# Projections from z1 by seven block products in segments 1 to 3 of a hybrid trunk layer

## The chip, the cores and the metric

The kernel runs on one core of one Trainium2 chip. The metric is the device time of one execution in microseconds (us); of several runs the median counts.

## The reference

One layer on 2048 positions of width 1024, with 16 meta positions ahead of them. All in float32.

```python
h = concat([meta, x]); z = rmsnorm(h, norm1_g)
q, fl, iv, og, pin, ga, gb = split(z @ w_in)        # 1024, 1024, 512, 512, 512, 1024, 1024 columns
o_a = hgrn2_mixer(q, fl + b_f, iv, og, lb, head_norm_g)
o_b = pool_mixer(pin, w_pool, pool_scale)
mix = sigmoid(ga) * (o_a @ w_branch_a) + sigmoid(gb) * (o_b @ w_branch_b)
h = h + mix @ w_out
z = rmsnorm(h, norm2_g); u, v = split(z @ w_up)
h = h + (silu(causal_dwconv(u)) * v) @ w_down
return rmsnorm(h)[:, 16:]
```

`hgrn2_mixer` is a gated linear recurrence with 8 heads of 128 x 64 state: f = lb + (1 - lb) sigmoid(fl), S = diag(f) S + (1 - f) i^T, o = S^T silu(q); then an rms norm of o per head and a product with silu(og). `pool_mixer` takes causal means of 2, 4, 8 and 16 positions less the position itself, and a 128 x 128 product per group.

## The kernel before

The sequence is worked in four segments of 512 columns (`SEG`; segment 0 has the 16 meta columns too). Within a segment the stages follow in this order: values (L271), four head pairs (L554), pooling (L590), the per-head norm (L617), the output gate (L637), the branch gates (L655), the out projection (L718), and the MLP with its down product.

**Precision.** Each operand of a product is kept as two halves, hi (the value rounded to fp32r) and lo (the rest), and a product is three passes, hi*hi, hi*lo, lo*hi (`PASS`, L129). Weights come from DRAM as a block of 128 x 1024 (0.5 MB) by `split_weights` (L90): a DMA on SP's queue into a ring of three `raw` tiles, ACT's cast for hi (L96), DVE's subtract for lo (L97), into a ring of three `w` tiles.

**Projections from z1.** `proj` (L131) makes one block of 128 output columns: 8 blocks of K x 3 passes = 24 matmuls of 128x512 into one PSUM bank. Per segment there are 8 for f, 8 for q, 4 for pooling, 4 for the output gate and 16 for the two branch gates.

**A pair of heads** (L554): both f blocks, k = 1 - f, `decays` (L288: products of f over 8 positions, on DVE, with two reciprocals), q's two blocks, the first block of the next pair's f, then `all_scores` (L346: products of q and k with the decays on DVE, small score products `sp` on PE) and `chunks_out` (L385: state products `up`, states `sc`, output `op`).

**After the pairs.** Pool sums `win` and `dt` (L602, L606), a product `pp`, its split `ob`. Then the squares of the output are split (`oss`) and summed per head by `msb` (L626); `ms` (L630) and `rsqrt` (L164, ten operations on an 8 x 512 tile, each needing the one before) give 1/rms, split into `rss` (L633). For each pair p the output gate's projection gives `t` (L643), times `oraw` (L645), times `bc` (L650: rss spread over the partitions by PE, L649), split into `oa` (L651). The branch gates (L655) make per block of 128 columns two projections from z1, 12 matmuls from `oa`, 12 from `ob`, and `mix`.

**The MLP** of segments 1 to 3 already takes two blocks of 128 columns at a time in seven products instead of eight (`q_rest`, L793): z2 has seven column groups of 256 (four quarters and three of their sums), the weights have seven operands (a11, a12, a22 and the sums s1 to s4), each product is 12 matmuls of 128x256 into half of a bank `X` or `Y`. ACT copies half banks aside (`sx`, `sy`, L817 to L828), DVE adds them (L830, L835). The sums s1 to s4 of the MLP's weights are made once, in segment 0, and kept in DRAM.

```python
129  PASS = ((0, 0), (0, 1), (1, 0))
136  for k in range(nk):
137      for i, (wi, xi) in enumerate(PASS):
138          T.matmul(pt[:, :n], lhsT=w[:, wi, (kof + k) * P:(kof + k + 1) * P],
```

The order of the work on each engine comes from a tile scheduler that places the instructions by its own estimates; each engine then runs its list in order. Pools bound how far it can run ahead: `w` 3, `raw` 3, PSUM 5 + 3 banks, wide rows `am` 12, `t` rows 6, x rows 2.

Of the kernel before, what the change touches and what calls it, by code (L numbers as in the profile page):

```python
# [16 lines left out]
P = 128  # L17
# [32 lines left out]
def trunk_layer(ctx: ExitStack, tc: tile.TileContext, x, meta, wts, cst, gf, wpool, out):  # L50
# [93 lines left out]
    def rows_product(src, chunks, nk, consume, between=(), lo=None, hg=HG, on_raw=None):  # L144
# [3 lines left out]
        for k in range(nk):  # L148
# [63 lines left out]
    def norm1_chunk(src, m, off, dst):  # L212
        t = x_row()
        nc.sync.dma_start(out=t[:m], in_=src)
        ss = new_sums(m < P)
        for i in range(2):
            square_sums(ss[:m, i, 0:1], t[:m, i * 512:(i + 1) * 512], m)
        rs = inv_rms(ss, 1)
        V.tensor_scalar(out=t[:m], in0=t[:m], scalar1=rs[:m, 0:1], scalar2=None, op0=ALU.mult)
        return lambda: norm1_transposes(t, m, off, dst)  # L220

    def norm1_transposes(t, m, off, dst):
        for kk in range(0, KB, 4):
            tp = ps.tile([P, 512], F32, name="tp", tag="mm", bufs=MM)
            for j in range(4):
                T.transpose(out=tp[:, j * P:j * P + m], in_=t[:m, (kk + j) * P:(kk + j + 1) * P],
                            identity=ident[:m, :m])
            for j in range(4):
                k = kk + j
                split((dst[k][:, 0, off:off + m], dst[k][:, 1, off:off + m]), tp[:, j * P:j * P + m],  # L230
                      scale=col(C_G1, k))

# [21 lines left out]
    def norm1(s):  # L254

        dst, rest = [], {}

        def load(c):
            rest[c] = norm1_chunk(x[s * SEG + c * P:s * SEG + (c + 1) * P], P, c * P, dst)

        def step(c, ahead):
            if not dst:
                dst.extend(z_plain())
            rest.pop(c)()
            if ahead:
                load(ahead)
        wait = lambda: None
        return ([lambda: load(0), lambda: load(1)],
                [lambda: step(0, 2), lambda: step(1, 3), wait, lambda: step(2, 0), lambda: step(3, 0)], dst)

    def values(s, z1, lo=None, between=()):  # L271
# [244 lines left out]
    t_d = {j0: dram.tile([4, nj // 2, P, 512], F32, name=f"t_d{j0}") for (j0, nj) in GROUPS}  # L516
    for s in range(nseg):
        if s > 0:
            nxt[0] = V_AT
            vt = values(s, z1)  # L520
# [31 lines left out]

        f_next = None
        for p in range(PAIRS):  # L554
            f = f_next if p else wide("f")
            k, q = wide("k"), wide("q")
            for e in range(1 if p else 0, 2):
                forget(p, e, f)
            nxt[0] = 4 * p + 2
            A.activation(out=k, in_=f, func=AF.Identity, scale=-1.0, bias=one)  # L560
            dec = decays(f, 2 * W)
            for e in range(2):
                b = e * W
# [546 lines left out]
```

## Time and profile before

| | |
|---|---|
| median of 3 runs | 3046.56 us (3041.91 to 3046.71) |
| the profiled execution | 3041.42 us, span 3039.7 us |
| mean granted TensorE clock | 0.996 |
| PE (TensorE) busy | 2969.6 us, 98% |
| PE weight loads busy | 2568.6 us, 85% |
| DVE (VectorE) busy | 2187.4 us, 72% |
| ACT (ScalarE) busy | 1360.8 us, 45% |
| DMA | 483.36 MB, 159 GB/s |

An engine's share is its busy time over the span. The shares are means: a stage can be full on an engine whose mean is low. Matmuls overlap each other in the records, so one matmul's own duration says little; the distance of the starts of a long run of them does. The same holds, less, for DVE.

### The profile page before, as it was taken

The numbers are of one execution on the slowest core, as the hardware profiler recorded it, in microseconds if no ns is written. First come the engines' busy times: TensorE is split into PE (matmuls) and PEld (weight loads), VectorE is DVE, ScalarE is ACT, GpSimd is POOL, SyncE is SP. The second block draws the span as 40 slices with busy tenths as digits, with TensorE's granted clock in tenths as the row PEclk, the third lists the DMA queues.
The fourth block names the chain that finished last, engine by engine and source line by source line (L and its number), as shares of the span: only waits on it lengthen the run. The fifth ranks groups of instructions, "written<-read, shape, count | busy, mean of one in ns | idle before, by whom it ended". The sixth has DMA issues, their size and how long they took to land.

```text
span 3039.7 us, 53537 instructions
## 1 busy us (share of the span) xinstructions
PE 2969.6 (98%) x21526; PEld 2568.6 (85%) x21526; DVE 2187.4 (72%) x3754; ACT 1360.8 (45%) x2214; POOL 74.4 (2%) x180
## 2 busy tenths in 40 slices
PE   7999999999999999999999999999999999999998
PEld 6999978888877788899977778799887778889997
DVE  5875357667868735988887853698887884488888
ACT  4443234333533424655554332555464442365555
POOL 1000000000000000000000000000000000000000
PEclk9999999999999999999999999999999999999999
DMA  3112238777632224666552122566664222356664
GB/s 144 64 64 84 84 137 294 263 268 263 237 135 75 76 92 145 224 216 225 196 197 78 64 90 92 189 203 224 213 204 170 71 71 92 116 180 228 216 218 160
DMA packets 198492, 483.36 MB, mean 159 GB/s; under 512 B 19794, under 2 KB 19922, under 8 KB 198244
## 3 DMA queue, kind: packets, MB, share of 16 engines
q1 hardware_dynamic: 198244, 479.95, 46.2%
q8 instruction: 169, 2.77, 0.4%
q14 instruction: 79, 0.65, 0.1%
HBM read 413.81 MB, written 66.06 MB: 158 GB/s over the span
## 4 chain that ended last, share of the span: by engine, by line
PE 82%; DVE 8%; ACT 5%; DMA 3%; issue 1%; SPq 0%; DVEq 0%; ACTq 0%; POOL 0%; POOLq 0%
PE pt L138 34%; PE rp L158 11%; PE dp L894 10%; PE X L793 8%; PE pt L760 8%; PE Y L793 6%; DVE w L97 2%; DMA raw<-in_wts_dram 1%; ACT w L96 1%; PE sp L328 1%; DVE cv L745 1%; DMA raw<-s_d 1%; DVE xt L286 1%; PE op L423 1%; ACT ta L706 0%
## 5 line engine op out<-in xcount | busy, mean ns | idle before, releaser
L97 DVE TENSOR_TENSOR w<-raw,w 128x1024 fp32r<-128x1024 f32 x625 | 760.9, 1220 | 545.6 <-ACT w L96 541.6
L138 PE MATMUL pt<-z,w 128*128 128x512 f32 (+3 forms) x4800 | 949.9, 353 | 0.0
L96 ACT CAST w<-raw 128x1024 fp32r<-128x1024 f32 x629 | 657.8, 1047 | 574.2 <-PE rp L158 162.2
L138 PEld LDWEIGHTS pt<-z,w 128*128 128x128 f32 x4800 | 769.6, 188 | 135.7 <-issue 11.8
L793 PE MATMUL X<-z,w 128*128 128x256 f32 x2484 | 338.6, 284 | 12.5 <-DVE z L123 4.2
L894 PE MATMUL dp<-w,act 128*128 128x512 f32 x1386 | 334.1, 397 | 11.4 <-DVE w L97 5.0
L793 PEld LDWEIGHTS X<-z,w 128*128 128x128 f32 x2484 | 313.9, 191 | 18.3 <-DVE z L123 5.9
L894 PEld LDWEIGHTS dp<-w,act 128*128 128x128 f32 x1386 | 257.7, 189 | 75.3 <-DVE w L97 8.7
L760 PE MATMUL pt<-z,w 128*128 128x256 f32 (+2 forms) x1608 | 253.7, 320 | 0.0
L760 PEld LDWEIGHTS pt<-z,w 128*128 128x128 f32 x1608 | 229.1, 190 | 23.2
L793 PE MATMUL Y<-z,w 128*128 128x256 f32 x1692 | 233.3, 284 | 2.5 <-ACT sy L826 2.3
L793 PEld LDWEIGHTS Y<-z,w 128*128 128x128 f32 x1692 | 214.7, 192 | 5.2 <-ACT sy L826 4.9
L158 PE MATMUL rp<-w,mix 128*128 128x512 f32 (+1 forms) x816 | 190.3, 394 | 0.0
L158 PEld LDWEIGHTS rp<-w,mix 128*128 128x128 f32 (+1 forms) x816 | 147.8, 182 | 40.1 <-issue 4.7
L661 ACT ACTIVATE sg<-pt 128x512 f32<-128x512 f32 (+1 forms) x80 | 41.2, 515 | 238.9 <-PE pt L138 238.9
L745 DVE SCALAR_TENSOR_TENSOR cv<-ub,cs,cv 128x512 f32<-128x512 f32 x176 | 131.4, 747 | 1.7
L902 DVE TENSOR_TENSOR h<-h,dp 128x512 f32<-128x512 f32 x192 | 124.4, 681 | 9.0 <-PE dp L894 8.9
L158 PE MATMUL rp<-w,act 128*128 128x512 f32 x528 | 123.6, 394 | 0.0
L158 PEld LDWEIGHTS rp<-w,act 128*128 128x128 f32 x528 | 98.9, 188 | 22.6
L748 ACT ACTIVATE sg<-cv 128x512 f32<-128x512 f32 x88 | 55.6, 632 | 113.5 <-DVE cv L745 113.3
L158 PE MATMUL rp<-w,z 128*128 128x512 f32 (+1 forms) x408 | 100.3, 404 | 0.0
L793 PE MATMUL X<-z,wa 128*128 128x256 f32 x684 | 95.6, 281 | 1.5 <-DMA wa<-a_d 1.5
(210 smaller groups left out, 3254.1 us busy)
## 6 DMA issues: line engine op xcount, KB each, us to landing
raw<-in_wts_dram SPq DMA_DIRECT2D x349, 512.0 KB, 3.5
raw<-s_d SPq DMA_DIRECT2D x264, 256.0 KB, 3.3
wa<-a_d SPq DMA_DIRECT2D x114, 512.0 KB, 4.9
raw<-in_wts_dram SPq DMA_DIRECT2D x183, 256.0 KB, 3.3
raw<-t_d SPq DMA_DIRECT2D x132, 256.0 KB, 2.9
a_d<-w SPq DMA_DIRECT2D x44, 512.0 KB, 3.7
s_d<-ws SPq DMA_DIRECT2D x44, 512.0 KB, 4.2
t_d<-ws SPq DMA_DIRECT2D x44, 256.0 KB, 2.2
```

The costliest lines, as they stand in the source:

```text
L96: A.copy(out=w[:, 0, :n], in_=raw[:, :n])
L97: (lo or V).tensor_tensor(out=w[:, 1, :n], in0=raw[:, :n], in1=w[:, 0, :n].bitcast(F32), op=ALU.subtract)
L138: T.matmul(pt[:, :n], lhsT=w[:, wi, (kof + k) * P:(kof + k + 1) * P], rhs=src[k][:, xi, c0 + o:c0 + o + n], start=(k == 0 and i == 0), sto ...
L158: T.matmul(banks[ci][:n, :], lhsT=src[k][:, xi, o:o + n], rhs=w[:, wi, (k % 2) * 512:(k % 2 + 1) * 512], start=(k == 0 and i == 0), stop=( ...
L286: mul = lambda o, a, b: V.tensor_tensor(out=o, in0=a, in1=b, op=ALU.mult)
L661: A.activation(out=sg[:, o:o + n], in_=pt[:, :n], func=AF.Sigmoid)
L745: V.scalar_tensor_tensor(out=cv, in0=ub[:, t_:t_ + SEG], scalar=col(C_CW + t_ * NF, j), in1=cv, op0=ALU.mult, op1=ALU.add)
L748: A.activation(out=sg, in_=cv, func=AF.Sigmoid)
L760: T.matmul(pt[:, po:po + n], lhsT=w[:, wi, k * P:(k + 1) * P], rhs=z2[k][:, xi, c0:c0 + n], start=(k == 0 and i == 0), stop=(k == KB - 1 a ...
L793: T.matmul(dst, lhsT=w[:, wi, kp * P:(kp + 1) * P], rhs=z2[kp][:, xi, xslot], start=(start and kp == 0 and i == 0), stop=(kp == KP - 1 and ...
L894: T.matmul(banks[i], lhsT=ops[kp][left][:, xi, i * P:(i + 1) * P], rhs=ws[kp][:, wi, :], start=(start and kp == 0 and n == 0), stop=(kp == ...
L902: V.tensor_tensor(out=v, in0=v, in1=banks[i], op=ALU.add)
```

## The change

In segments 1 to 3 all projections from z1 but the values go two blocks at a time through `quad`, seven products of 12 matmuls of 128x256: per segment 4 quads for f, 4 for q, 2 for pooling, 2 for the output gate, 8 for the branch gates (ga and gb of one block make one quad). Segment 0 keeps the old form.

- z1 gets the seven column groups (`z_first`, `z_half`, `z_sums`). `norm1` transposes rows 0 and 1 first, rows 2 and 3 later; the sums of z1 are made inside the values' product, as is the final norm (`finish`) of the segment before, which stood at that segment's end.
- f and q: segment 0 writes a11, a12 and a22 split (hi and lo) to DRAM (`keep`), and in the branch gates' loop the sums (`keep_sums`): s2 and s1 split, s3 and s4 not. Later segments load them; only s3|s4 are split on the chip.
- pooling, output gate and branch gates: `block_op` loads the two raw blocks, makes four sums of 512 on DVE (`block_sums`) and four splits (of 1024, 1024, 1024 and 512).

```diff
+    def block_sums(ru, rg, t0, t1):
+        a11, a12, a21, a22 = ru[:, :512], ru[:, 512:], rg[:, :512], rg[:, 512:]
+        s2, s1, s3, s4 = t0[:, :512], t0[:, 512:], t1[:, :512], t1[:, 512:]
+        V.tensor_tensor(out=s1, in0=a21, in1=a22, op=ALU.add)
+        V.tensor_tensor(out=s3, in0=a21, in1=a11, op=ALU.subtract)
+        V.tensor_tensor(out=s2, in0=s1, in1=a11, op=ALU.subtract)
+        V.tensor_tensor(out=s4, in0=a12, in1=s2, op=ALU.subtract)
...
+        def p1():
...
+            seventh(z, bank["X"][:, HT:], op("a11"), B11, True)
+        def p2():
+            seventh(z, bank["Y"][:, :HT], op("a12"), B21, True)
+            A.copy(out=sx[:, :HT], in_=bank["X"][:, HT:])
+        def p6():
+            seventh(z, bank["X"][:, HT:], op("s2"), T2, False)
+        def p5():
+            seventh(z, bank["Y"][:, HT:], op("s1"), T1, True)
+            A.copy(out=sx[:, HT:], in_=bank["X"][:, HT:])
+        def p7():
+            seventh(z, bank["X"][:, HT:], op("s3"), T3, False)
+            A.copy(out=sy[:, HT:], in_=bank["Y"][:, HT:])
+        def p3():
+            seventh(z, bank["Y"][:, HT:], op("s4"), B22, False)
+            A.copy(out=sy[:, :HT], in_=bank["X"][:, HT:])
+            V.tensor_tensor(out=sx, in0=bank["Y"], in1=sx, op=ALU.add)
+            out0()
+        def p4():
+            seventh(z, bank["X"][:, :HT], op("a22"), T4, True)
+            V.tensor_tensor(out=sy, in0=bank["X"], in1=sy, op=ALU.add)
+            out1()
+        return [p1, p2, p6, p5, p7, p3, p4]
...
-            vt = values(s, z1)
+            vt = values(s, z1_part, between=[z1_sums, lambda: finish(0, NCH)])
...
+        def qf_op(i):
...
+            nc.sync.dma_start(out=ws.bitcast(F32), in_=cs_d[i])
+            wr = split_weights(cr_d[i])[0]
...
+        def block_op(iu, temp):
+            ru, rg = load_raw(wts[iu]), load_raw(wts[iu + 1])
+            wn = split_tile(ru)
+            t0, t1 = temp(), temp()
+            block_sums(ru, rg, t0, t1)
+            w0, w1, w2 = split_tile(t0), split_tile(t1), split_tile(rg[:, 512:])
...
+                run(query_steps(p, q))
+                if p + 1 < PAIRS:
+                    f_next, steps = forget_steps(p + 1)
+                else:
+                    steps = pool_steps(0)
+                run(steps, 0, 4)
...
+                    run(quad(z1, block_op(4 * PAIRS + 4 + p, am_row), og[0], og[1], lambda: gate(0), lambda: gate(1), "mm"))
...
+                keep_sums(d)
...
+                run(quad(z1, block_op(nxt[0], x_row), gates[0][:, :W], gates[1][:, :W], lambda: gate(0), lambda: gate(1), "hg"))
```

The scheduler's order moves with it. The first place is PE's list in segment 1 around the sums of squares `msb` and the spread `bc`. Before (pt from z and w is a projection of the output gate):

```order
L138 MATMUL pt<-z,w 128x512 x2
L626 MATMUL msb<-oss,ind 8x512 x2
L138 MATMUL pt<-z,w 128x512
L626 MATMUL msb<-oss,ind 8x512
L138 MATMUL pt<-z,w 128x512 x60
L649 MATMUL bc<-rss,indT 128x512 x6
L138 MATMUL pt<-z,w 128x512 x2
L649 MATMUL bc<-rss,indT 128x512 x2
L138 MATMUL pt<-z,w 128x512 x48
L138 MATMUL pt<-oa,w 128x512 x12
```

and now (X and Y from z and w are the banks of a quad):

```order
L774 MATMUL pp<-dt,wp 128x512
L127 MATMUL X<-z,w 128x256 x5
L127 MATMUL Y<-z,w 128x256 x12
L774 MATMUL pp<-dt,wp 128x512 x2
L819 MATMUL msb<-oss,ind 8x512 x8
L856 MATMUL bc<-rss,indT 128x512 x6
L127 MATMUL X<-z,w 128x256 x2
L127 MATMUL Y<-z,w 128x256 x2
L127 MATMUL X<-z,w 128x256 x10
L127 MATMUL Y<-z,w 128x256 x10
L127 MATMUL X<-z,w 128x256 x12
L127 MATMUL Y<-z,w 128x256 x12
```

Before, 60 projections stand between msb and bc; now nothing does: the two steps of the first output-gate quad that are ready without sums (p1 and p2, the 24 matmuls ahead of msb) stand before it.

The second place is DVE's list at the same point, from `ms` to `rss`. Before:

```order
L630 TENSOR_SCALAR ms<-msb 8x512
L166 TENSOR_SCALAR rs<-ms 8x512
L169 SCALAR_TENSOR_TENSOR n_10519<-rs 8x512
L170 TENSOR_TENSOR n_10520<-n_10519,ms 8x512
L643 SCALAR_TENSOR_TENSOR t_10544<-pt,cs,t_10544 128x512
L171 SCALAR_TENSOR_TENSOR rs<-n_10520,rs 8x512
L645 TENSOR_TENSOR t_10544<-t_10544,oraw 128x512
L169 SCALAR_TENSOR_TENSOR n_10519<-rs 8x512
L643 SCALAR_TENSOR_TENSOR t_10584<-pt,cs,t_10584 128x512
L170 TENSOR_TENSOR n_10520<-n_10519,ms 8x512
L645 TENSOR_TENSOR t_10584<-t_10584,oraw 128x512
```

and now (L258 to L263 are the rsqrt, bs the sums s1 to s4 of a weight block):

```order
L262 TENSOR_TENSOR n_11166<-n_11165,ms 8x512
L263 SCALAR_TENSOR_TENSOR rs<-n_11166,rs 8x512
L261 SCALAR_TENSOR_TENSOR n_11165<-rs 8x512
L262 TENSOR_TENSOR n_11166<-n_11165,ms 8x512
L263 SCALAR_TENSOR_TENSOR rs<-n_11166,rs 8x512
L113 TENSOR_TENSOR bs<-raw 128x512
L114 TENSOR_TENSOR bs<-raw 128x512
L215 TENSOR_TENSOR rss<-rs,rss 8x512
L115 TENSOR_TENSOR bs<-bs,raw 128x512
L116 TENSOR_TENSOR bs<-raw,bs 128x512
L101 TENSOR_TENSOR w<-bs,w 128x1024 x2
```

Before, the rsqrt's operations alternate with those of the output gate; now they stand together, and the first output-gate quad's sums s2 and s4 and its subtracts follow rss.

The third place is DVE's list behind that, at the output gate. Before:

```order
L645 TENSOR_TENSOR t_10624<-t_10624,oraw 128x512
L650 TENSOR_TENSOR t_10544<-t_10544,bc 128x512
L650 TENSOR_TENSOR t_10584<-t_10584,bc 128x512
L650 TENSOR_TENSOR t_10624<-t_10624,bc 128x512
L123 TENSOR_TENSOR oa<-t_10544,oa 128x512
L123 TENSOR_TENSOR oa<-t_10584,oa 128x512
L123 TENSOR_TENSOR oa<-t_10624,oa 128x512
L643 SCALAR_TENSOR_TENSOR t_10664<-pt,cs,t_10664 128x512
```

and now (t is the gate of a block, L113 to L116 are the sums of the second output-gate quad):

```order
L848 SCALAR_TENSOR_TENSOR t_11185<-t_11185,cs,sg 128x512
L163 TENSOR_TENSOR t_11186<-X,t_11186 128x512
L852 TENSOR_TENSOR t_11185<-t_11185,oraw 128x512
L857 TENSOR_TENSOR t_11185<-t_11185,bc 128x512
L848 SCALAR_TENSOR_TENSOR t_11186<-t_11186,cs,sg 128x512
L215 TENSOR_TENSOR oa<-t_11185,oa 128x512
L852 TENSOR_TENSOR t_11186<-t_11186,oraw 128x512
L857 TENSOR_TENSOR t_11186<-t_11186,bc 128x512
L113 TENSOR_TENSOR bs<-raw 128x512
L114 TENSOR_TENSOR bs<-raw 128x512
L215 TENSOR_TENSOR oa<-t_11186,oa 128x512
L115 TENSOR_TENSOR bs<-bs,raw 128x512
```

The second quad's sums, which its third step needs, stand behind the results of the first.

## Rows read from the trace of the kernel before

**Rows 1.** The page: busy time of the engines, and the chain that ended last.

```profile
PE 2969.6 (98%) x21526; PEld 2568.6 (85%) x21526; DVE 2187.4 (72%) x3754; ACT 1360.8 (45%) x2214; POOL 74.4 (2%) x180
...
PE 82%; DVE 8%; ACT 5%; DMA 3%; issue 1%; SPq 0%; DVEq 0%; ACTq 0%; POOL 0%; POOLq 0%
```

**Rows 2.** The chain by pieces, segment 1's gates: start, length (us), what.

```profile
1036.27 133.44 PE pt L138 x576
```

**Rows 3.** The same view, MLP of segment 2, first pieces of two quads.

```profile
2060.59 2.84 PE X L793 x24
...
2100.83 0.24 PE X L793 x2
```

**Rows 4.** Busy time by window, segment 1: length, each engine's busy time, clock, DMA.

```profile
856.24:965.73 109.49, 109.05 (x1273) 85.79 (x1271) 85.38 (x181) 45.84 (x70) 0.20 (x1) 1.00 0.23 77
965.73:1033.20 67.47, 66.90 (x568) 51.02 (x566) 55.58 (x104) 27.57 (x43) 2.33 (x7) 1.00 0.21 70
1033.20:1047.40 14.20, 14.20 (x59) 10.73 (x59) 9.36 (x14) 5.15 (x8) 0.00 (x0) 1.00 0.19 60
1047.40:1169.71 122.31, 122.31 (x530) 99.26 (x529) 45.50 (x51) 34.73 (x44) 0.00 (x0) 1.00 0.28 97
915.99:948.01 32.02, 31.80 (x411) 24.85 (x410) 26.47 (x59) 13.48 (x21) 0.20 (x1) 1.00 0.20 68
...
1020.00:1036.20 16.20, 16.20 (x68) 12.11 (x67) 15.20 (x24) 4.76 (x7) 0.00 (x0) 1.00 0.30 98
```

(The columns behind the length are PE, PE's weight loads, DVE, ACT and POOL.)

**Rows 5.** Groups of DVE instructions by line: busy time, mean of one (ns).

```profile
L97 DVE TENSOR_TENSOR w<-raw,w 128x1024 fp32r<-128x1024 f32 x48 | 58.6, 1222 | 76.2 <-ACT w L96 76.2
...
L667 DVE TENSOR_TENSOR sg<-sg 128x512 f32<-128x512 f32 x7 | 4.8, 693 | 0.2
...
L126 DVE SCALAR_TENSOR_TENSOR z<-tp,cs,z 128x128 fp32r<-128x128 f32 x27 | 8.6, 344 | 2.1 <-ACT z L125 2.1
```

**Rows 6.** Timeline of DVE in the rsqrt of segment 1: start, duration, instruction.

```profile
1021.10 0.68 DVE L169 SCALAR_TENSOR_TENSOR n<-rs 8x512 f32<-8x512 f32 x1
1021.81 0.68 DVE L170 TENSOR_TENSOR n<-n,ms 8x512 f32<-8x512 f32 x1
...
1023.68 0.67 DVE L645 TENSOR_TENSOR t<-t,oraw 128x512 f32<-128x512 f32 x1
1024.29 0.67 DVE L169 SCALAR_TENSOR_TENSOR n<-rs 8x512 f32<-8x512 f32 x1
```

**Rows 7.** Timeline of DVE, wide and narrow operations of two pairs.

```profile
982.30 1.22 DVE L286 TENSOR_TENSOR k<-k,tt 128x1024 f32<-128x1024 f32 x1
983.43 1.22 DVE L97 TENSOR_TENSOR w<-raw,w 128x1024 fp32r<-128x1024 f32 x1
...
965.75 0.37 DVE L411 SCALAR_TENSOR_TENSOR sc<-st,tt,up 128x64 f32<-128x64 f32 x2
966.04 0.27 DVE L411 SCALAR_TENSOR_TENSOR sc<-sc,tt,up 128x64 f32<-128x64 f32 x1
```

**Rows 8.** Busy time by window, two quads of segment 1's MLP.

```profile
1322.89:1343.00 20.11, 20.11 (x170) 20.06 (x170) 17.23 (x25) 11.72 (x21) 0.61 (x4) 1.00 0.73 242
```

**Rows 9.** Groups of ACT instructions in the same window: cast and half-bank copy.

```profile
L96 ACT CAST w<-raw 128x1024 fp32r<-128x1024 f32 x5 | 5.3, 1052 | 2.3 <-PE X L793 1.6 <-ACT sy L828 0.8
...
L817 ACT COPY sx<-X 128x256 f32<-128x256 f32 x2 | 0.7, 366 | 1.0 <-PE X L793 1.0
```

**Rows 10.** Windows and PE timeline at the end of segment 1.

```profile
1540.00:1542.20 2.20, 0.66 (x4) 0.42 (x4) 2.20 (x9) 1.76 (x4) 0.00 (x0) 1.00 0.38 137
1542.20:1545.00 2.80, 2.79 (x8) 2.17 (x9) 2.65 (x13) 1.42 (x5) 0.00 (x0) 0.59 0.88 292
...
1542.21 6.96 PE L894 MATMUL dp<-w,act 128*128 128x512 f32 x22 [1.38 <-DVE nrm L166]
```

**Rows 11.** Windows at the boundaries into segments 2 and 3.

```profile
1520.00:1570.00 50.00, 44.91 (x229) 36.02 (x228) 47.43 (x124) 34.22 (x79) 0.19 (x1) 0.97 0.43 145
...
2260.00:2310.00 50.00, 44.30 (x217) 35.01 (x218) 47.96 (x125) 34.68 (x80) 0.19 (x1) 1.00 0.48 160
```

More of the change, by code (lines that the diff above doesn't have):

```diff
@@ L254, in norm1, with first, second, sums @@
     def norm1(s):
-        dst, rest = [], {}
+        z, ta, b12, rows = [], [], [], {}
         def load(c):
[L259 to L266, printed above, removed]
+            t = rows[c] = x_row()
+            nc.sync.dma_start(out=t, in_=x[s * SEG + c * P:s * SEG + (c + 1) * P])
+            ss = new_sums(False)
+            for i in range(2):
+                square_sums(ss[:, i, 0:1], t[:, i * 512:(i + 1) * 512], P)
+            rs = inv_rms(ss, 1)
+            V.tensor_scalar(out=t, in0=t, scalar1=rs[:, 0:1], scalar2=None, op0=ALU.mult)
+        def first():
+            z_first(z, ta, rows, C_G1)
+            load(2)
+            load(3)
+        def second():
+            for kp in range(KP):
+                z_half(ta[kp], kp, rows, 1, C_G1)
+                b12.append(vpl.tile([P, 2, HT], F32R, name="b12", tag="vt"))
+                split((b12[kp][:, 0], b12[kp][:, 1]), ta[kp][:, 1])
+                split((z[kp][:, 0, B22], z[kp][:, 1, B22]), ta[kp][:, 3])
+        def sums():
+            for kp in range(KP):
+                z_sums(z[kp], ta[kp], x_row().rearrange("p (u t) -> p u t", t=HT))
+        def part(k, xi, o):
+            kp = k % KP
+            t = z[kp][:, xi, B21 if k >= KP else B11] if o < HT else z[kp][:, xi, B22] if k >= KP else b12[kp][:, xi]
+            return t[:, o % HT:o % HT + P]
         wait = lambda: None
-        return ([lambda: load(0), lambda: load(1)],
-                [lambda: step(0, 2), lambda: step(1, 3), wait, lambda: step(2, 0), lambda: step(3, 0)], dst)
+        return [lambda: load(0), lambda: load(1)], [first, wait, wait, wait, second], z, part, sums
     def values(s, z1, lo=None, between=()):
@@ L553, in trunk_layer, with run @@
+        def run(steps, a=0, b=7):
+            for f_ in steps[a:b]:
+                f_()
         f_next = None
         for p in range(PAIRS):
-            f = f_next if p else wide("f")
+            if s == 0:
+                f = f_next if p else wide("f")
+                for e in range(1 if p else 0, 2):
+                    forget(p, e, f)
+            elif p:
+                f = f_next
+                run(steps, 4)
+            else:
+                f, steps = forget_steps(0)
+                run(steps)
@@ L833, in q_rest @@
             cv, sg = conv(j, ub)
[L834 removed]
+            seventh(z2, X[:, :HT], take(), 6, True)
             V.tensor_tensor(out=sy, in0=X, in1=sy, op=ALU.add)
```

266 lines of the change are left out of this document (167 added, 99 removed).

## The prediction, before the change was run

> **What bounds the kernel now.** I first read the page's busy shares and its chain of the work that ended last: TensorE (PE) is busy 98% of the span and makes 82% of the chain, VectorE (DVE) is busy 72% [rows 1]. On average, then, fewer PE columns should mean less time. Next the chain piece by piece. In the gates of segment 1, 576 matmuls of 128x512 run back to back in 133.44 us, 0.2317 us each [rows 2]. In the MLP of segment 2, which already works by seven block products, one such unit starts every 10.06 us ((2100.83 - 2060.59) / 4) and has 84 matmuls of 128x256, 0.1197 us each [rows 3]. So a quad costs PE 10.06 us where two projections cost 48 x 0.2317 = 11.12: 1.06 us saved. The change makes 60 quads (20 in each of segments 1 to 3: 4 for f, 4 for q, 2 pool, 2 output gate, 8 branch gates): **63.8 us at most**, if PE never waits.
>
> The third view, busy time by stage, says where it may wait [rows 4]. I cut segment 1 at four marks: (a) first projection to the third pair's state products, (b) from there to rss (the per-head 1/rms, ready), (c) rss to the first product from oa, (d) the other gates. PE fills all four (109.05 of 109.49, 66.90 of 67.47, 14.20 of 14.20, 122.31 of 122.31). DVE is at 78, 82, 66 and 37% of them. Stage (b) is the one with little DVE to spare.
>
> **What the change costs DVE.** A split's subtract of 128x1024 is busy 1.22 us, a 512-wide add 0.69, a 128-wide operation 0.34 [rows 5]. Starts lie closer than that: two 1024-wide operations 1.13 us apart, two of 64 in 0.29 [rows 7]; 512-wide ones 0.71 us apart where the second needs the first (1021.10 to 1021.81), 0.60 where not (1023.68 to 1024.29) [rows 6]. I price by starts: 0.65 for a 512-wide operation, 1.13 for a 1024-wide one.
> - f and q quads: 2 adds from PSUM in, one split of two out (a11, a12, a22, s2, s1 come split from DRAM). About even, 2 x 0.65 - 1.13 = +0.2 us. Each loads 3 MB for 1 MB. At a pair's two quads in some 31 us that is 190 GB/s over today's other loads; the MLP moves 242 GB/s at a DMA share of 0.73 with PE full [rows 8]. Nothing on the path. If this cover fails, a quad waits for its operands (rival 3).
> - pool, output-gate and branch-gate quads: 2 adds, 4 sums of 512, splits of 1024, 1024, 1024 and 512 for two of 1024: 7 x 0.65 + 1.13 = **+5.7 us** each, 12 in a segment.
>
> [...]
>
> **Segment 1, stage by stage** (2 and 3 repeat it).
>
> (a) 109.5 us. At most 6.5 quads x 1.06 = 6.9 us go. But each pair has a chain (f's last step, sigmoid, k, decays, products for k and q, first scores) that PE covers with q's two projections and half of the next f: 72 x 0.2317 = 16.7 us before, one quad and four steps of seven, 10.06 + 5.75 = 15.8, after. DVE is already at 26.47 of 32.02 us per pair [rows 4]. I take half: **-3.6**.
>
> (b) 67.5 us. The order (front part) shows the change here: 60 of the output gate's projections covered the rsqrt chain (ms, then ten dependent operations to rss) on PE; now PE has two steps of the first quad ahead of msb and nothing behind it. So the end of (b) is set by DVE, in order: 62 operations of 512 (40.3), 8 of 1024 (9.0), 16 of 128 at 0.35 (5.6), 17 of 64 at 0.14 (2.4), 3 predicated copies and small ones (1.5): 58.8 us, with some 3 us of waits for ACT and PE that DVE can't fill: 62. **-5.5**: projections have left this stage, so it gets shorter though PE idles in it.
>
> (c) 14.2 us. After rss: the sums s2 and s4, ACT's cast of s2|s1 (1.05 [rows 9]) and its subtract (1.13) before the first quad's third step: 3.2 us. Five steps of 12 x 0.1197: 7.2. Then the second quad's sums stand on DVE behind the first quad's results (L163, then gate, oraw and bc multiplies, oa for both blocks): 12 operations x 0.65, one subtract of 1.13, and about 1.3 of ACT's sigmoid and cast between them: 10.3, while PE has only two steps (2.9) to do. Five steps more: 7.2. The first branch-gate quad: 10.06. Sum 38.0: **+23.8**. The bounds: DVE packed without a gap, 33 x 0.65 + 9 x 1.13 = 31.6 (+17.4); every hop of ACT exposed and busy means in place of starts, 42 (+28).
>
> (d) 122.3 us. PE-bound: 7 quads x 10.06 + 8 x 24 x 0.2317 = 114.9. A round's DVE work is 4 sums, four subtracts (three of 1024, one of 512) and out's weights, 2 adds, 3 gate operations and mix: 11.5 of 15.6 us, so it hides, and the sums run one quad ahead. **-7.4**.
>
> Sum +7.3 per segment.
>
> **The clock after a gap.** [...] Two gaps of this kind come per segment, the rsqrt chain (about 9 us) and the second output-gate quad (about 7): +3.8. [...] That makes **+11.1 per segment, +33 for three**.
>
> **The rest.** At two boundaries (into segments 2 and 3) PE lacks about 5 us of 50 with DVE at 47 to 48 [rows 11]. The new norm replaces 32 subtracts of 128 by 4 of 512 and 8 of 256, some 4 us less DVE ahead of the values; the sums of z1 (4 x (0.65 + 2 x 0.4 + 1.13) = 10 us) run beside the values' 23 us on PE, and the first quad needs them only at its third step. Bounds 0 and -5 each; I take -2.5 each, -5. Where the norm is late, the values' product waits. Segment 0 gains 8 x (4 x 0.65 + 1.13) = 30 us of DVE and 16 us of SP's writes, under stages that PE fills; their price lies between 0 and +5, I take +1. The finish that moves into the values is DVE work under PE.
>
> Sum: 33 - 5 + 1 = +29 on the profiled execution's 3041.4 us, 3070.4. The median of the runs shown is 5.1 us above that execution, so **3075 us**.
>
> **The rivals.**
> 1. DVE packs. The order is fixed but not the gaps: if ACT's answers are always there, (b) is 58.8 and (c) 31.6, and if the clock does not fall, a segment gets -3.6 - 8.7 + 17.4 - 7.4 = -2.3; three make -7, with -5 and +1 a time of 3030.5, in the runs' median **3036**: faster. The deciding point is (c): without clock loss the change breaks even where (c) is about 32. For it: before, DVE is busy 15.20 of 16.20 us around rss [rows 4]. Against: there the chain was interleaved with independent work, now its ten operations follow each other at 0.71. 13%.
> 2. PE stays full after all: 60 x 1.06 = 64 us less, **2983**. It would need the sums of the second output-gate quad well before their place in the order. The PE column of [rows 4] speaks for it, the order against. 4%.
> 3. The quads themselves wait in the mixer: the third step writes the half bank that ACT must have copied (0.37 us) within the 1.44 us of the second step, and a cast of 1.05 may stand before it [rows 9]; or an operand from DRAM is late. 0.8 us for each of 60 is +48: **3123**. Against it: the MLP's quads have the same copies and casts, and PE is at 20.11 of 20.11 [rows 8]. 8%.
> 4. The gains and (c) cancel: within 0.2% of 3046.6 (3040.5 to 3052.7), about what a measurement of this kernel can tell from no change. 9%.
>
> **How the numbers follow.** The forecast has the remaining 66%: slower, 3053 to 3106 with (c) between 34 and 42 and 0 to 4 us of clock loss a segment. Chances: faster 0.17 (rivals 1 and 2), same 0.09, slower 0.74. The range leaves out rival 2, most of rival 3 and the lower half of rival 1: **3038 to 3106**.
>
> **What would show it.** Right: in segment 1 after the change, a PE gap of about 9 us that ends with bc, released by DVE's rss; a second of some 7 us before the second output-gate quad's third step, released by a DVE subtract; 35 us or more from rss to the first oa product; rounds of 15.6 us in the other gates; quads of 10.0 to 10.1 us there. Wrong: (c) under 32 us, a clock of 1.00 right after both gaps, or quads over 10.5 us each in the gates, which would be rival 3.

## The result, and the profile after

The changed kernel took 3095.85 us (median of 4 runs, 3093.31 to 3101.61), the kernel before in the same comparison 3046.64: a ratio of 1.0165, with a 95% interval of 1.0144 to 1.0185. It is 49 us slower. The forecast was 3075, slower, with 3038 to 3106 as its range: direction and mechanism hold, but the forecast loss was 28 us and the measured one is 1.7 times that. The profiled execution took 3096.68 us with a span of 3094.9, 55.2 us more than the span before.

The page of the changed kernel, busy times and chain, answers to [rows 1]:

```profile
PE 2949.8 (95%) x23686; PEld 2671.5 (86%) x23686; DVE 2427.2 (78%) x4094; ACT 1497.3 (48%) x2498; POOL 75.6 (2%) x180
...
PE 77%; DVE 13%; ACT 4%; DMA 3%; issue 2%; SPq 0%; DVEq 0%; ACTq 0%
```

PE is busy only 19.8 us less than before, where 60 quads were to save 63.8. The saved work is there: PE is busy at a granted clock of 0.50 for 100.4 us in all, for 10.9 before, and half of that difference and the 19.8 make 64. But 55 us more have passed: PE waits for some 75 us more. DVE has 240 us more to do and 13% of the chain instead of 8%. The mean granted clock fell from 0.996 to 0.975.

The four stages of segment 1 of the changed kernel, by window (length, PE, weight loads, DVE, ACT, POOL, clock, DMA share, GB/s), answer to the first four of [rows 4]:

```profile
864.09:971.76 107.67, 104.13 (x1559) 98.54 (x1559) 86.17 (x191) 49.86 (x92) 0.85 (x4) 1.00 0.63 223
971.76:1037.08 65.32, 48.23 (x575) 39.15 (x571) 57.36 (x109) 26.02 (x48) 1.10 (x4) 0.85 0.13 42
1037.08:1078.18 41.10, 35.60 (x237) 33.15 (x237) 33.47 (x46) 20.22 (x33) 0.00 (x0) 0.82 0.28 80
1078.18:1193.08 114.90, 114.90 (x783) 106.50 (x781) 84.90 (x109) 57.32 (x87) 0.00 (x0) 1.00 0.34 108
```

Stage (d), PE-bound, gained what 1.06 us a quad promises. In (b) and (c) PE, which filled them before, is busy 83.8 of 106.4 us, and both show a clock below 1.00. The two kernels cut at the same marks (the start of bc stands for rss; "rest" runs to the next segment's first projection), in us, before and after:

| stage | segment 1 | segment 2 | segment 3 | forecast |
|---|---|---|---|---|
| (a) | 109.7, 107.7 | 109.7, 109.5 | 109.6, 108.3 | -3.6 |
| (b) | 67.5, 65.3 | 67.2, 64.7 | 67.2, 66.6 | -5.5 |
| (c) | 14.1, 41.1 | 14.1, 41.2 | 14.1, 42.2 | +23.8, and +3.8 for the clock |
| (d) | 122.1, 114.9 | 122.2, 115.1 | 122.2, 115.0 | -7.4 |
| rest | 423.5, 420.6 | 420.8, 417.1 | 399.5, 401.6 | -2.5 at two boundaries |

Segment 0, up to the first projection of segment 1, took 8 us more: 4.1 up to its out projection, 3.9 behind that.

The longest waits of PE in segment 1's (a) to (c) in the changed kernel (who waited for what: us in total, times, longest):

```profile
PE bc L856 <- ACT rss L214: 8.3, 1, 8.3
PE X L127 <- ACT w L100: 7.1, 2, 5.4
PE pp L774 <- DVE dt L799: 3.9, 2, 3.0
```

These are the two gaps of the forecast, and a third ahead of them that it did not have. PE's timeline there (start, length, instruction, idle before and what ended it):

```profile
1015.59 1.60 PE L127 MATMUL Y<-z,w 128*128 128x256 f32 x12
1018.16 1.10 PE L774 MATMUL pp<-dt,wp 128*128 128x512 f32 x2 [0.97 <-DVE dt L799]
1022.22 2.08 PE L774 MATMUL pp<-dt,wp 128*128 128x512 f32 x2 [2.96 <-DVE dt L799]
...
1037.08 2.92 PE L856 MATMUL bc<-rss,indT 8*128 8x512 f32 x6 [8.29 <-ACT rss L214]
1039.93 0.80 PE L127 MATMUL X<-z,w 128*128 128x256 f32 x2
...
1041.18 2.50 PE L127 MATMUL X<-z,w 128*128 128x256 f32 x10
...
1045.40 1.60 PE L127 MATMUL X<-z,w 128*128 128x256 f32 x12
...
1048.29 3.04 PE L127 MATMUL X<-z,w 128*128 128x256 f32 x24
...
1058.85 0.79 PE L127 MATMUL X<-z,w 128*128 128x256 f32 x2 [5.43 <-ACT w L100]
...
1060.11 2.38 PE L127 MATMUL X<-z,w 128*128 128x256 f32 x10
...
1063.52 1.60 PE L127 MATMUL X<-z,w 128*128 128x256 f32 x12
...
1066.40 3.04 PE L127 MATMUL X<-z,w 128*128 128x256 f32 x24
```

The Y row at 1015.59 is p2 of the first output-gate quad; its third step starts at 1039.93, 23 us later, after pp, msb and bc. The five terms of (c) can be read off, a step being 12 x 0.1197 us at the full clock: bc to the first quad's third step 2.85 us (forecast 3.2); its five steps to 1049.73, 9.80 (7.2, the clock apart); to the second quad's third step 9.12 (10.3); its five steps to 1067.84, 8.99 (7.2); the first gate quad to 1078.18, 10.34 (10.06). The sum is 41.1. Both gaps end with a cast on ACT (rss, w), one hop behind the DVE operation that the forecast named; DVE's subtract then holds each quad's fifth matmul, which starts 1.29 and 1.28 us after the subtract does (1041.18 and 1060.11).

DVE's timeline shows its waits in the pool stage and why the second quad waits: everything stands in one list.

```profile
1025.05 0.75 DVE L218 SCALAR_TENSOR_TENSOR ob<-pp,cs,ob 128x512 fp32r<-128x512 f32 x1 [1.69 <-ACT ob L217]
1026.59 1.29 DVE L215 TENSOR_TENSOR oss<-osq,oss 128x512 fp32r<-128x512 f32 x2 [0.79 <-ACT oss L214]
1028.82 0.68 DVE L823 TENSOR_SCALAR ms<-msb 8x512 f32<-8x512 f32 x1 [0.94 <-PE msb L819]
...
1039.89 2.36 DVE L101 TENSOR_TENSOR w<-bs,w 128x1024 fp32r<-128x1024 f32 x2 [0.39 <-ACT w L100]
...
1050.60 0.69 DVE L163 TENSOR_TENSOR t<-X,t 128x512 f32<-128x512 f32 x1
1051.20 0.68 DVE L852 TENSOR_TENSOR t<-t,oraw 128x512 f32<-128x512 f32 x1
...
1055.23 0.69 DVE L113 TENSOR_TENSOR bs<-raw 128x512 f32<-128x512 f32 x1
...
1057.03 0.69 DVE L115 TENSOR_TENSOR bs<-bs,raw 128x512 f32<-128x512 f32 x1
1057.76 0.69 DVE L116 TENSOR_TENSOR bs<-raw,bs 128x512 f32<-128x512 f32 x1
1058.83 2.36 DVE L101 TENSOR_TENSOR w<-bs,w 128x1024 fp32r<-128x1024 f32 x2 [0.38 <-ACT w L100]
```

The second quad's sums start at 1055.23, behind the results of the first, and the subtract that its third step needs starts at 1058.83, behind ACT's cast.

The granted clock around the gaps, by window:

```profile
1010.00:1015.00 5.00, 5.00 (x34) 4.01 (x32) 4.46 (x8) 0.76 (x2) 0.52 (x2) 1.00 0.00 0
1015.00:1020.00 5.00, 3.29 (x20) 2.28 (x18) 4.75 (x8) 1.40 (x3) 0.19 (x1) 1.00 0.02 3
1020.00:1025.00 5.00, 2.78 (x5) 0.96 (x6) 3.33 (x6) 2.71 (x6) 0.00 (x0) 0.62 0.00 0
...
1030.00:1040.00 10.00, 2.92 (x7) 1.84 (x7) 9.30 (x15) 1.81 (x3) 0.00 (x0) 0.50 0.00 0
1040.00:1045.00 5.00, 4.98 (x22) 4.68 (x23) 2.86 (x3) 1.70 (x3) 0.00 (x0) 0.50 0.58 157
1045.00:1050.00 5.00, 5.00 (x43) 5.00 (x43) 1.98 (x3) 2.32 (x4) 0.00 (x0) 0.99 0.13 52
```

In segment 1 the clock was 0.50 from 1021.2 us, in the pool stage's waits and before the rsqrt began (1029.54), to 1045.1, when the first quad had run for about 5 us; segment 2 is alike (0.50 from 1772.2 to 1796.1). In segment 3 it was back at 1.00 for 3.4 us (2526.5 to 2529.9) as the rsqrt began and fell to 0.50 again within it. What it costs (c) is less than the slow matmuls suggest, because part of them is hidden. The first quad's third and fourth steps, 24 matmuls, take 5.47 us (1039.93 to 1045.40) where 24 x 0.1197 = 2.87, but the fifth of them had to wait for DVE's first subtract in any case (it starts at 1039.89, the fifth matmul at 1041.18). From there 20 matmuls take 4.22 us for 2.39, 1.83 more. In the second quad they take 3.41 (1060.11 to 1063.52), 1.02 more. bc's six, also slow (2.92 us at 0.50, 1.65 at 1.00 in the version with the gates alone by quads), cost little or nothing: the third step's operand comes from ACT's cast, for which DVE's row at 1039.89 waited too. So the clock costs some 2.9 us of (c), an estimate from these rows, where 3.8 was taken for a segment; the same count gives 3.0 and 4.0 in segments 2 and 3.

### The profile page after: what moved, and what is told of

It reads as the page before. It is cut to its first block, busy times and chain, and to the rows that moved or that the text cites. A ratio compares the mean times of both kernels' runs of the same rounds, so it can differ in the third digit from the quotient of the medians.

```text
span 3094.9 us, 58864 instructions
## 1 busy us (share of the span) xinstructions
PE 2949.8 (95%) x23686; PEld 2671.5 (86%) x23686; DVE 2427.2 (78%) x4094; ACT 1497.3 (48%) x2498; POOL 75.6 (2%) x180
## 4 chain that ended last, share of the span: by engine, by line
PE 77%; DVE 13%; ACT 4%; DMA 3%; issue 2%; SPq 0%; DVEq 0%; ACTq 0%
PE X L127 17%; PE pt L230 13%; PE Y L127 12%; PE rp L250 12%; PE dp L1079 10%; PE pt L957 8%; DVE w L101 2%; DMA raw<-in_wts_dram 2%; DVE q L377 1%; ACT w L100 1%; DVE k L377 1%; DVE cv L942 1%; PE sp L419 1%; PE sp L431 1%; DMA xt<-in_x_dram 1%
## 5 line engine op out<-in xcount | busy, mean ns | idle before, releaser
L101 DVE TENSOR_TENSOR w<-raw,w 128x1024 fp32r<-128x1024 f32 (+1 forms) x601 | 713.0, 1188 | 369.3 <-ACT w L100 353.8
L100 ACT CAST w<-raw 128x1024 fp32r<-128x1024 f32 (+1 forms) x605 | 618.0, 1023 | 504.8 <-DMA raw<-in_wts_dram 110.0
L127 PE MATMUL X<-z,w 128*128 128x256 f32 x4788 | 667.1, 288 | 38.8 <-ACT w L100 20.8
L127 PEld LDWEIGHTS X<-z,w 128*128 128x128 f32 x4788 | 616.4, 194 | 58.4 <-ACT w L100 24.7
L127 PE MATMUL Y<-z,w 128*128 128x256 f32 x3564 | 499.5, 287 | 2.9 <-ACT sy L1011 2.9
L127 PEld LDWEIGHTS Y<-z,w 128*128 128x128 f32 x3564 | 460.4, 194 | 8.5 <-ACT sy L1011 5.3
L957 PEld LDWEIGHTS pt<-z,w 128*128 128x128 f32 x1608 | 229.1, 190 | 23.2
L230 PE MATMUL pt<-z,w 128*128 128x264 f32 (+2 forms) x1920 | 249.0, 288 | 0.0
L230 PEld LDWEIGHTS pt<-z,w 128*128 128x128 f32 x1920 | 238.5, 191 | 3.5 <-issue 1.6
L127 PE MATMUL Y<-z,wa 128*128 128x256 f32 x972 | 131.4, 282 | 0.0
L127 PEld LDWEIGHTS X<-z,wa 128*128 128x128 f32 x972 | 126.2, 190 | 3.6 <-issue 1.6
```

Of the source, the lines that this page charges most:

```text
L100: A.copy(out=w[:, 0, :n], in_=src)
L101: (lo or V).tensor_tensor(out=w[:, 1, :n], in0=src, in1=w[:, 0, :n].bitcast(F32), op=ALU.subtract)
L127: T.matmul(dst, lhsT=w[:, wi, kp * P:(kp + 1) * P], rhs=z[kp][:, xi, xslot], start=(start and kp == 0 and i == 0), stop=(kp == KP - 1 and ...
L957: T.matmul(pt[:, po:po + n], lhsT=w[:, wi, k * P:(k + 1) * P], rhs=z2[k][:, xi, c0:c0 + n], start=(k == 0 and i == 0), stop=(k == KB - 1 a ...
```

## The experiments

The theory: the loss sits at the output gate, where the sums and subtracts made in place stand in DVE's order, the rsqrt has nothing on PE to cover it, and the clock falls. The rivals: quads lose in themselves, wherever they stand; only the amount of DVE work counts; f's and q's kept operands cost. Executions of one kernel differ by up to 14 us here, so for a version with a single run the stages, which repeat in three segments, say more than the time.

**Output gate direct.** The edit in segments 1 to 3 (`proj_z1` is `proj` on the quarters of z1; the fourth quarter is kept by four ACT copies a segment):

```diff
-            if s == 0:
+            if True:
...
-                for (o, n), pt in zip(pb, proj(w, 0, KB, z1, c1, pb)):
+                for (o, n), pt in zip(pb, proj(w, 0, KB, z1, c1, pb) if s == 0 else proj_z1(w)):
```

> The output gate of segments 1 to 3 goes back to direct projections (24 matmuls for 8 K blocks, the columns in two pieces because z1 now lies in quarters); all other quads stay, and the fourth quarter of z1 is kept by four copies of ACT a segment. Theory (the loss sits at the output gate: its two quads' sums and subtracts stand in DVE's order behind the rsqrt and behind each other's results, PE has nothing to cover them, and TensorE's clock falls in the gap): stages (b) and (c) of segment 1, 65.3 + 41.1 us in the changed kernel, fall to 80 to 86 together, 60 projections stand between msb and bc again, the clock of (c) is near 1.00, and the time is 3015 to 3040, below the kernel before. Rival (quads lose in themselves, in the mixer, wherever they stand): the gap moves to the pool quads or the first gate quad and the time stays at 3070 to 3095.

It took 3038.61 us, ratio 0.9979 (0.9970 to 0.9989): 57 us of the loss are gone by two quads of twenty in a segment, and the kernel is a little faster than before, as expected. In the profiled executions 51 us of that lie in (b) and (c), and 4 in a stretch of segment 0 that the edit does not touch (last section). That carries the place the theory names and ends the rival that quads lose wherever they stand. The stages were not as expected: (b) and (c) together are 90.5, 88.5 and 90.7 us for 80 to 86, PE still waits 3.2 us before bc, and the clock still falls (0.69 in (c)). Windows of (b) and (c) in segment 1:

```profile
968.14:1043.25 75.11, 67.20 (x713) 59.42 (x709) 68.43 (x122) 33.76 (x58) 1.11 (x4) 0.95 0.27 85
1043.25:1058.62 15.37, 15.37 (x81) 13.08 (x81) 10.38 (x17) 6.47 (x12) 0.00 (x0) 0.69 0.15 43
```

DVE is busy for 91% of (b): the pool quads' sums are still there.

**The same quads, written earlier.** The output-gate quads stand ahead of the squares in the program, and their results lie in wide rows instead of `t` rows; nothing else differs:

```diff
+        for p in range(0, PAIRS if s else 0, 2):
+            t = blk.tile([P, 2 * WMAX], F32, name="t1", tag="am", bufs=12)
...
+            run(quad(z1, block_op(4 * PAIRS + 4 + p, am_row), og[p], og[p + 1], lambda: gate(0), lambda: gate(1), "mm"))
         msb = [ps.tile([P, 512], F32, name="msb", tag="hg", bufs=HG) for _ in pb]
```

> The same quads and the same sums in place as in the changed kernel; only the output-gate quads are written ahead of the squares and the rsqrt in the program, with their results in wide rows. Theory (order, not amount): the sums leave the stretch behind rss, so (c) falls from 41 to 16 to 22 us, but DVE's work in (b) + (c), 90.8 us busy, stays, so together they fall only from 106 to 92 to 98; the time falls by 25 to 45, to 3050 to 3070. Rival (amount of DVE work alone): no change, 3090 to 3100. Rival (quads lose in themselves): no change either, with PE waiting inside the early quads.

One run, 3076.53 us. In segment 1 (c) falls to 12.6 us, further than expected, but (b) rises to 87.7; together they are 100.3, 100.4 and 102.2 for 106.4, 105.9 and 108.8 in the changed kernel, where 92 to 98 was expected, and the time lies above its range. So order alone is worth some 6 us a segment, 18 in all, about a third of what the direct form gives. That is more than the rivals' nothing. The rsqrt still leaves PE idle for 4.5 us, and a split still holds a quad for 3.7:

```profile
PE X L127 <- ACT w L100: 5.4, 2, 3.7
PE bc L857 <- ACT rss L214: 4.5, 1, 4.5
PE msb L830 <- ACT oss L214: 3.3, 2, 3.1
```

**Output gate from kept operands.** The quads stay, their operands are made in segment 0 and kept in DRAM:

```diff
-                    run(quad(z1, block_op(4 * PAIRS + 4 + p, am_row), og[0], og[1], lambda: gate(0), lambda: gate(1), "mm"))
+                    run(quad(z1, og_op(2 * PAIRS + p // 2), og[0], og[1], lambda: gate(0), lambda: gate(1), "mm"))
...
+                if d >= KB - 2:
+                    keep_sums(d + 2)
```

> The output gate keeps its quads, but their operands come from DRAM as those of f and q do: segment 0 writes them split (two more sets of sums in its gate loop), later segments load 3 MB a quad and split one tile. Theory: what costs is the sums made in place at this point of DVE's order, not the quad; (b) + (c) falls from 106 to 80 to 88 us and the time to 3015 to 3045, near that of the direct form. Rival 1 (quads lose in themselves): 3070 to 3095. Rival 2 (DMA: 3 MB a quad comes late): PE waits in (c) end with a DMA from the kept operands, 10 us a segment, and the time is 3050 to 3080.

3072.28 us, ratio 1.0090 (1.0068 to 1.0113): outside what the theory gave, and in the ranges of both rivals. (b) and (c) are 95.2, 95.6 and 98.9 us, some 10 below the changed kernel, but the out projection of segment 0 began at 407.0 us for 391.9: the added sums and writes cost 15 us there, once. Without these 15 the time would still be above 3045. In segment 1 PE's waits at this place are for splits (ACT w 4.3 us, DVE w 2.0), for rss (2.9) and for the kept operands' DMAs (1.6, not the 10 of rival 2). So the sums and three of the four splits, which go with them, are worth about 10 us a segment, and the quads without them still stand 5 to 8 us above the direct form: at this place a quad does lose something in itself, as rival 1 said of all of them. The waits point to the split that is left; no run takes it away.

**Pool direct, output gate by quads.**

```diff
...
-            elif g == 0:
-                run(steps, 4)
-            elif g == 2:
-                run(pool_steps(2))
+            if g:
+                pool_in(g)
```

> Only the two pool quads of a segment go back to direct projections; the output gate keeps its quads. Theory (DVE's work sets (b) and (c)): the pool quads' sums and subtracts, 2 x 5.7 us, leave (b), which falls from 65 to 56 to 61; (c) stays at 40 to 42 with both gaps; the time falls by 12 to 27, to 3069 to 3084. Rival (the rsqrt gap alone sets it, not the amount of DVE work ahead): (b) stays at 64 to 66, the time at 3090 to 3100.

One run, 3083.89 us; (b) is 61.8, 62.7 and 62.3, (c) 41.8 to 42.2. Both gaps stay (8.3 and 5.4 us) and the time is at the upper end of what was expected, but (b) fell less than to 56 to 61. In segment 1 DVE is busy 9.8 us less in it (57.4 before this edit):

```profile
970.11:1031.88 61.77, 47.48 (x562) 38.05 (x557) 47.55 (x93) 22.46 (x40) 2.10 (x7) 0.92 0.17 53
```

Of that 3.5 us come back; DVE's longest waits there are now for the last pair's products on PE (`up` 2.7 us, `sp` 2.3 and 2.0). So the amount of DVE's work alone does not set (b).

**f and q direct.** Nothing is kept in DRAM:

```diff
...
+            for e in range(2):
+                b = e * W
+                w = weights()
+                for (o, n), pt in zip(pa, proj(w, 0, KB, z1, 0, pa) if s == 0 else proj_z1(w)):
...
-                run(query_steps(p, q))
-                if p + 1 < PAIRS:
-                    f_next, steps = forget_steps(p + 1)
...
```

> f and q direct in all segments, nothing kept in DRAM for them; pool, output gate and branch gates as in the changed kernel. Theory: (a) 110.5, 1 to 3 us more a segment; (b) + (c) still 104 to 109, so the loss does not come from f and q; segment 0 gives back what its writes and sums cost (0 to 8 us): 3088 to 3104. Rival (the kept operands' 3 MB a quad or the added PSUM adds of f and q push everything behind them): (b) + (c) falls under 95 and the time under 3070.

One run, 3089.34 us, as expected; (a) 110.4 to 111.1, (b) and (c) 105.5 to 106.0. f's and q's quads are not the cause of the loss. Their sixteen blocks of a segment gain only 2 us in (a), and the time without them is not longer but 6.5 us shorter: in its profile segment 0 gives back 3.6 us, the rests of the segments 6, (b) and (c) 4.

**Pool and output gate direct, f, q and gates by quads** (both edits above).

> Pool and output gate direct; f, q and branch gates by quads, their sums for f and q from DRAM. Theory: (b) + (c) 80 to 83, as with the gates alone by quads (81.3), (a) 107 to 109, (d) 115; some 2 us a segment below the kernel with the gates alone, less what segment 0 pays for keeping the operands: 3005 to 3020, the fastest so far or level with 3018. Rival (f's and q's quads delay the pairs): (a) 111 or more, 3020 to 3035.

3027.43 us, ratio 0.9930 (0.9911 to 0.9947). (a) 108.2 to 110.1, (b) and (c) 85.6 to 85.8, above the 80 to 83 expected, and the time above the range and in the rival's, though (a) is not the 111 that the rival asked for. PE comes to bc before DVE and ACT have rss; the gap before bc is 2.2 us, and behind it the clock of (c) is 0.68:

```profile
1027.21 9.33 PE L174 MATMUL pt<-z,w 128*128 128x512 f32 x63
1036.38 1.60 PE L127 MATMUL X<-z,w 128*128 128x256 f32 x12
1040.18 0.96 PE L870 MATMUL bc<-rss,indT 8*128 8x512 f32 x3 [2.20 <-ACT rss L225]
```

**Only the branch gates by quads.** All else direct, nothing kept:

> Of the quads only the eight of the branch gates stay; f, q, pooling and output gate are direct again (columns in two pieces), and segment 0 keeps nothing. Theory: (d) stays at 115 us, (a) goes back to 109.6 to 111, (b) + (c) to 80 to 82; 7 to 9 us less a segment than before and some 3 at two boundaries, 3015 to 3030. Rival (the new norm and the sums of z1 cost what the gates give): 3040 to 3050.

3018.51 us, ratio 0.9916 (0.9899 to 0.9933), as expected: 0.8% faster than the kernel before, and the fastest here by its median; its interval overlaps that of the version above. Its four stages in segment 1, and PE's rows before bc, from the fastest of its four runs (3009.26 us):

```profile
857.66:968.14 110.48, 109.91 (x1448) 96.57 (x1446) 84.92 (x182) 46.03 (x71) 0.23 (x1) 1.00 0.27 84
968.14:1036.62 68.48, 68.08 (x679) 57.78 (x679) 57.19 (x107) 27.50 (x43) 2.40 (x7) 1.00 0.20 63
1036.62:1049.57 12.95, 12.95 (x96) 11.88 (x96) 10.96 (x17) 7.66 (x14) 0.00 (x0) 1.00 0.43 134
1049.57:1164.57 115.00, 115.00 (x782) 106.58 (x781) 84.60 (x109) 57.50 (x87) 0.00 (x0) 1.00 0.33 107
...
1022.32 14.37 PE L174 MATMUL pt<-z,w 128*128 128x512 f32 x95
1036.62 1.65 PE L856 MATMUL bc<-rss,indT 8*128 8x512 f32 x6
```

PE is full in all four, and the clock is 1.00 in each: 95 matmuls of direct projections run into bc without a gap.

**Filling the gap, twice.** The changed kernel with products on PE that nobody reads, tied to the rsqrt's operations.

```diff
+            dm = ps.tile([P, 512], F32, name="dm", tag="hg", bufs=HG)
+            rsqrt(rs, ms, n1, n2, lambda t: T.matmul(dm, lhsT=t[:, :P], rhs=t, start=True, stop=True))
```

> The changed kernel with ten small products added on TensorE in segments 1 to 3, one behind each operation of the per-head rsqrt (its tile of 8 x 512 with itself, into a bank that nothing reads); nothing else moves, and the output is the same. They keep TensorE at work through the rsqrt gap. Theory (part of (c) is the clock: 0.82 granted there): the granted clock of the first output-gate quad goes back to 1.00, its five steps take 7.2 to 8.5 us instead of 11.5, (b) stays within 1 us; (c) falls from 41 to 35 to 38 and the time by 8 to 18 us, to 3078 to 3088. The second gap (5.4 us) stays. Rival (those steps are slow because ACT's copies and DVE's subtracts come late): no change, or some us slower by the added products.

One run, 3120.31 us, 24 us slower where the theory had it 8 to 18 faster. The products, of 8 rows in fp32, ran longer (1.71 us each, start to start) than the operations they were tied to and held the chain up: its operations start 1.71 us apart for 0.71, (b) is 74.9 us for 65.3, (c) 42.2.

```diff
+            def seen(t):
+                T.matmul(dm[:, :64], lhsT=t[:, :P], rhs=t[:, :64], start=True, stop=True)
+                for k in range(2):
+                    T.matmul(dm, lhsT=z1[0][:, 0, B11, :P], rhs=z1[k][:, 0, B21:B22 + 1].rearrange("p u t -> p (u t)"),
+                             start=True, stop=True)
```

> The fill once more, with work of another kind: behind each of the ten rsqrt operations one short product of that tile (64 columns) and two full products of z1 with itself (128 rows, 128x512, fp32r), 20 in all, into a bank that nothing reads; the output is the same. At 0.23 us each they fit between the operations, which start 0.71 us apart, so DVE's chain should not wait. In the first fill the products of 8 rows held the chain up (10.9 us became 18.5) and the clock stayed at the lower level, so it told nothing of the clock's price. Theory (5 to 6 us of (c) are the clock): the clock is back at 1.00 by bc, the first quad's third and fourth steps take 2.9 us for 5.5, bc's six matmuls 1.7 for 2.9; (c) falls from 41 to 35 to 38, (b) is 65 to 67, the time 3078 to 3092. Rival (the steps wait for ACT and DVE, not the clock): (c) stays at 40 to 42 and the time at 3093 to 3102.

3126.17 us, ratio 1.0265 (1.0232 to 1.0297), outside both ranges: (b) is 76.6 us in segment 1, (c) 40.9. Again the chain waited for the fill (1.09 us before each of the last four operations in segment 1). In segments 1 and 3 the first two full products take 0.73 us (1029.57 and 2551.84), in segment 2 they take 1.22 (1791.02), as all the later ones do in all three. In segment 1 the fill begins at 1029.21 us, and the clock by window is:

```profile
1020.00:1025.00 5.00, 3.13 (x5) 1.04 (x6) 3.28 (x6) 2.71 (x6) 0.00 (x0) 0.50 0.00 0
1025.00:1030.00 5.00, 3.04 (x10) 0.86 (x8) 3.62 (x7) 2.11 (x5) 0.00 (x0) 0.82 0.00 0
1030.00:1035.00 5.00, 5.00 (x14) 2.99 (x12) 3.14 (x5) 0.00 (x0) 0.00 (x0) 0.52 0.00 0
1035.00:1040.00 5.00, 5.00 (x13) 2.82 (x12) 1.74 (x4) 0.00 (x0) 0.00 (x0) 0.50 0.00 0
1040.00:1045.00 5.00, 5.00 (x13) 2.69 (x12) 4.58 (x7) 2.71 (x4) 0.00 (x0) 0.50 0.07 13
```

At 0.50 one group took 1.77 us, not 0.7. Neither fill kept the clock up (0.79 and 0.82 in (c) of segment 1), so neither tests it. The 5 to 6 us that the expectation put on the clock were read without the wait for DVE's subtract; the 2.9 us of (c) above are read from rows at either level in the changed kernel and not shown by an edit that restores the clock.

**What follows together.** By the ratios the way from the changed kernel to the one with the gates alone is 0.0249, some 76 us: 0.0186 (57 us) when the output gate goes direct, 0.0049 (15 us) for pooling on top, and 0.0014 (4 us, within the intervals) for f, q and the kept operands. The first and the last hold some 4 us each of the stretch of segment 0 that the last section shows. Shown is the place: the output gate's two quads, in (b) and (c). There the direct form is worth 17 us a segment, of which order alone gives 6, and the sums with three of four splits 10; the last split's and the clock's parts are read from waits and rows. Eight of the twenty quads clearly earn their place, the ones in a stage where PE is full with DVE at 37% before the change.

## Why the prediction was right, and where it was undersized

- **The price of a quad** (1.06 us on PE): right. (d) fell by 7.2 us, forecast 7.4.
- **The output gate**, step (c): right in place, order and size. Forecast 38.0 and 3.8 for the clock, 41.8; measured 41.1, 41.2, 42.2, of which the clock is some 2.9, 3.0 and 4.0, so the rest is 38.2 in each. That it meets the forecast to 0.2 us is in part luck: the second quad's wait was 9.1 us for 10.3, and inside each quad's steps some 0.8 us of waiting for DVE's subtract make up for it. The packed DVE of rival 1 (31.6) did not come, and the direct form removed the loss. The deciding point named there, about 32, was passed by 9 us.
- **The clock**: 3.8 us a segment were taken, two falls at 1.9 us each. No run shows 1.9 for both: [rows 10] have one stretch of 22 matmuls in 6.96 us where 22 x 0.2317 is 5.10, and in (c) of segment 1 the two falls cost 1.8 and 1.0, so the size was about right. Where the first starts was not: in segments 1 and 2 in the pool stage's waits, not in the rsqrt, so that part of (b) runs at the lower clock too, which the forecast had at nothing (two `pp` take 2.08 us at 1022.22 for 1.10 at 1018.16).
- **(b)**: the gain was put too high. Forecast -5.5, measured -2.2, -2.5 and -0.6. The list of DVE operations was right (57.4 us busy for 58.8 forecast). The step that failed is the "some 3 us of waits": DVE stands idle for 8 of the 65.3 us. Nearly half of that lies where pooling, squares and `ms` answer each other on DVE, ACT and PE (1.69 for `ob`, 0.79 for `oss`, 0.94 for `msb`, and 0.4 for Y), the rest in the last pair. Taking the pool quads out does not remove the waits (3.5 us of 9.8 came back), so what would is open.
- **(a)**: the gain was put too high. Half of 6.9 us was taken; 2.0, 0.2 and 1.3 came. PE is busy some 5 us less, but it waits for 3.5, 5.4 and 4.2 us, where before it waited for 0.4 or 0.5. In segment 2, 4.2 of the 5.4 stand before the first scores `sp`, the end of the chain that the forecast named and took half for. (a) and (b) together are missing some 18 us over three segments, most of the error of 26 in the span.
- **Segment 0**: +1 was taken, 8 us came. The sums and writes in the gates' loop cost nothing (126.5 us from its first product from oa to its out projection, before and after), as priced. No run shows the 16 us of SP's writes; in the trace 24 writes of 512 KB landed in a median of 3.4 us, 8 of 1024 KB in 6.3, 8 of 512 KB more in 3.8. 4 us are the clock's, in the last section; the other 3.9, behind the out projection, stay open.
- **Boundaries**: right in size, -2.9 and -3.7 for -2.5 each. The rest of segment 3, which has no boundary behind it and was put at nothing, is 2.1 us longer.
- **Rivals**: 1, 2 and 4 did not come. Of rival 3 nothing was found in the gates: rounds of 15.6 us, and PE at 114.90 of 114.90. In the mixer, where it was meant, the steps of the quads wait for 0.7 us in all in (a) of segment 1.
- **DVE priced by starts**: right. In this trace the operations of the rsqrt again start 0.71 us apart (1030.70 to 1031.41 and on), independent ones 0.60 (1036.30 to 1036.90); (b) was longer by its waits.

## What to carry to other kernels

A form that saves PE work pays where PE is full and the engine that feeds it has room, so price it by stage: the same quad earned 1 us in the gates and lost 8 to 9 at the output gate. Before moving work off PE, ask what that work was covering; here 60 matmuls of projections hid a chain of ten dependent operations. And read the new order of the feeding engine, since what it makes for the next product stands behind the results of the last.

## What the runs showed that was not expected

In segment 0 the changed kernel lost 4 us between bc and the first product from oa (22.7 us for 18.3) with the same PE instructions in the same order as before, and without a gap on PE. The granted clock accounts for it: 0.50 from 246.4 to 256.7 us in the changed kernel, and half of these 10.2 us is 5.1. Here from 243 to 252 us in the kernel before and in the changed one:

```profile
243.00:252.00 9.00, 9.00 (x58) 7.50 (x58) 7.21 (x15) 3.47 (x6) 0.00 (x0) 1.00 0.11 41
...
243.00:252.00 9.00, 9.00 (x40) 7.05 (x40) 5.53 (x13) 2.27 (x5) 0.00 (x0) 0.69 0.12 47
```

It was also 1.00 there in the versions with only the output gate direct and only the gates by quads, 0.70 in the one with pool and output gate direct and 0.67 in the one with f and q direct. What tells these apart stays open: PE alternates there between projections and small products of 8 rows in the kernel before (bc from 243.00 to 249.77) as in the changed one (242.75 to 251.76). There is one profile of each version, so it may as well differ from run to run: the four runs of the version with only the gates by quads lie between 3009 and 3021 us with mean clocks of 0.993 to 0.997, and its profile is of the fastest.

And PE was busy in the records without the full clock: in the second fill it was busy 5.00 of 5.00 us at 0.50, with two full products of 512 columns in every 1.77 us, each pair 1.22 us long, after a first pair of 0.73.
